# A mixture-of-experts layer: the last expert in the order is one of over 128 rows, and the norm of all tokens runs in pieces

## The chip, the core and the metric

One core of a Trainium2 chip runs the whole layer in one program. The metric is the time of one execution on the device in microseconds, the median of three runs. The profile is one further execution, taken by the hardware profiler. In the profile PE is TensorE's matrix products, PEld its weight loads, DVE VectorE, ACT ScalarE, POOL GpSimd and SP SyncE; L12 is line 12 of the kernel before.

## What is computed

A decoder layer for 512 tokens of width 1024: a token mixer (differential attention beside a gated branch), a norm, and then a mixture of 32 experts of which each token takes four. The end of the reference is what matters here:

```python
def moe_ffn(x, w_router, b_router, w_up, b_up, w_down, b_down):
    ...
    def expert_block(args):
        xb, e = args
        h = xb @ w_up[e] + b_up[e]
        gate, lin = h[:, :D_FF], h[:, D_FF:]
        gate = jnp.minimum(gate, SWIGLU_LIMIT)
        lin = jnp.clip(lin, -SWIGLU_LIMIT, SWIGLU_LIMIT)
        act = (lin + 1.0) * gate * jax.nn.sigmoid(SWIGLU_ALPHA * gate)
        return act @ w_down[e] + b_down[e]
    ...
# in reference():
x = layer_norm(DEEPNORM_ALPHA * x + mixed, ln1_g[l], ln1_b[l])
ffn = moe_ffn(x, w_router[l], b_router[l], w_up[l], b_up[l], w_down[l], b_down[l])
x = layer_norm(DEEPNORM_ALPHA * x + ffn, ln2_g[l], ln2_b[l])
```

The up weights of an expert are 8 MB, its down weights 4 MB.

## The kernel before

The first 290 us are the token mixer, the first norm and the routing. Then come the experts, in slots. An expert's rank by its number of tokens gives its capacity (`CAP_STEPS`, L35): the texts call an expert of at most 64 rows **narrow** (`L` in `ORDER`, L57), one of 72 to 128 rows **middle** (`M`) and one of 192 rows **wide** (`H`, the four fullest but for one fixed expert). `slot_order` (L61) takes the ranks in the order that `ORDER` writes out by hand. A middle expert multiplies with fp32r matmuls: each weight chunk is cast to a high part on ScalarE (L152) and its remainder is formed on VectorE (L153), into a ring of five buffers, and `full_mm` (L1342) makes six matmuls of 512 columns from it. A narrow expert multiplies the raw weights in f32, each row's two halves of 512 columns on the two halves of the array (`half_mm`, L1331): nothing is cast. A wide expert does both: 128 rows as a middle one and 64 more as a narrow one, the latter with PD as the place of its up product and X1 as that of its down product.

The work list (L1400 to L1405) is up(n), down(n-1), up(n+1), down(n) and so on; at its end stand down(N-2), up(N-1), down(N-1). It is cut into chunks (`stream`): 16 for an up product, 8 for a down product. Four chunks use one weight part of 2 MB; an expert has six parts, four up and two down. There are six raw buffers, and SyncE issues the next load when a buffer is released (`used`, L1563; `issue_load`, L1417): after the last split of a middle expert's part, after the last matmul of a narrow or wide one's. The program order on every engine is the order of emission (`manual_schedule`). Behind chunk c first the splits are emitted up to `limit(c + 1)` (L1591), which is three chunks ahead where something is hung in, then what `at(c, ...)` has hung in behind that chunk. So an instruction hung in behind chunk c stands on ScalarE and VectorE behind the splits of the next three chunks and ahead of all others.

Results are added to a tensor in DRAM, `accd`, which starts with the tokens themselves (L1121): `out_a` (L1310) scales an expert's rows by their gates into a buffer of `ys` and `out_b` (L1322) scatters them with an adding DMA of GpSimd (L1169, L1216). The last expert of before is narrow and different. Its gates are spread to all partitions (`last_diag`, `last_mm`, `last_gates`, L1655 to L1673) and multiplied into the transposed activations; the accumulator's rows for its tokens are gathered (`summed`, L1610) and put into its PSUM bank by a matmul with the identity (`last_start`, L1675), on which the down product then adds; so its PSUM holds finished sums. `last_rows` (L1680) takes their norm and scatters the result into the output. The norm of all tokens takes the accumulator without the last expert: `ln2_sums` behind the up product, `ln2_squares`, `ln2_scaled` and `ln2_out` behind the down product's second chunk (L1704 to L1711). It writes all 512 rows of the output, and the scatter of `last_rows` then overwrites those that the last expert has changed. `full_list` (L1183) makes the list of the last expert so that empty places repeat its first row. Behind the stream stands a loop over what did not fit the capacities (L1746), with no turn here.

Of the kernel before, what the change touches and what calls it, by code (L numbers as in the profile page):

```python
# [11 lines left out]
I32 = mybir.dt.int32  # L12
# [44 lines left out]
ORDER = "LMLHLMLMLMLHLMLMLMLHLMLMMLMLHLL"  # L57
assert "HH" not in ORDER and "MH" not in ORDER and ORDER[-1] == "L"
# [9 lines left out]
def moe_layer(ctx, tc, x, w_in, lambda_q1, lambda_k1, lambda_q2, lambda_k2, subln_g, gmlp_ln_g,  # L68
# [775 lines left out]

    def list_cols(lp, rows, dst=None):
# [326 lines left out]
    def transpose_h(src, eng, dst=None, js=slice(0, 4)):  # L1172

        if dst is None:
            dst = view(words(f"low{nxt('tb', 4)}", 1024), 0, 8, 64)
        tp = xbank().rearrange("p (j r) -> p j r", j=4)
        sv = src.rearrange("p (q j) -> p q j", j=4)
        for j in range(js.start, js.stop):
            nc.tensor.transpose(tp[:, j], sv[:, :, j], ident)
        eng(dst.rearrange("p (c j) r -> p j c r", c=2)[:, js], tp.rearrange("p j (c r) -> p j c r", c=2)[:, js])  # L1180
        return dst

    def full_list(s):  # L1183

        lp = xbank()[:, 0:8].rearrange("p (n c) -> p n c", n=2)
        for n in range(2):
            for i in range(NT):
                cols = tb.oh[:, i, 0:1].to_broadcast([128, 128]) if n else tb.oh[:, i]
                nc.tensor.matmul(lp[:, n], cols, tb.R[:, i, s], start=(n == 0 and i == 0), stop=(n == 1 and i == 3))
        cols_ = words("r0", 16)  # L1190
        t = view(cols_, 0, 2, 4)
        empty, gt, idx = (view(cols_, 8 + n, 1) for n in range(3))
        idx = idx.bitcast(I32)
        nc.vector.tensor_copy(t, lp)
        nc.vector.tensor_scalar(empty, t[:, 0, 1:2], -1.0, 1.0, op0=OP.mult, op1=OP.add)
        nc.vector.scalar_tensor_tensor(t[:, 0], t[:, 1], empty, t[:, 0], op0=OP.mult, op1=OP.add)
        nc.vector.scalar_tensor_tensor(idx, t[:, 0, 0:1], 2.0, bge[:, 2:3], op0=OP.mult, op1=OP.add)
        nc.vector.tensor_tensor(gt, t[:, 0, 2:3], t[:, 0, 3:4], op=OP.add)
        return idx, gt
# [21 lines left out]
    class Slot:  # L1221
# [3 lines left out]
        def __init__(self, n, s):  # L1225
# [8 lines left out]
            assert not (self.last and self.full)  # L1234
# [21 lines left out]
        def fetch(self, b):  # L1256
            if self.last:
                self.lists[b] = full_list(self.s)
            elif self.is_half(b):
# [20 lines left out]
        def t_a(self, b, hf):  # L1280
            if self.last:
                def gated(to, tp):
                    nc.vector.tensor_tensor(to, tp, tb.last_gates.unsqueeze(1).unsqueeze(1).to_broadcast([128, 2, 2, 64]),
                                            op=OP.mult)
                self.aT[b] = transpose_h(self.act_rows(b), gated, self.aT[b], slice(2 * hf, 2 * hf + 2))
            elif self.is_half(b):
# [7 lines left out]
        def act(self, b, q):  # L1294

            v = (self.act_rows(b),) + ((self.hg, self.hl) if self.is_half(b) else (PG[0:self.full], PL[0:self.full]))
            if self.last:
                return [a.rearrange("p (q j) -> p q j", j=4)[:, :, 2 * q:2 * q + 2] for a in v]
# [11 lines left out]
        def out_a(self):  # L1310
# [6 lines left out]
            for b in range(self.nparts):  # L1317
                half = self.is_half(b)
                self.y[b] = y_buf()[:, 0:512] if half else y_buf()[0:self.full]
# [11 lines left out]
        def half_mm(self, P, T, k, w, started=False):  # L1331
            for c in range(2):
                nc.tensor.matmul(P[64 * c:64 * c + 64], T[:, k], w[:, c * 512:(c + 1) * 512],  # L1333
                                 start=(k == 0 and not started), stop=(k == 7))
# [45 lines left out]
        def down_chunks(self):  # L1380
            out_ = []
            for k in range(KT):
                def mm(w, hi, lo, k=k):
# [4 lines left out]
                    if self.half:  # L1388
                        self.half_mm(self.hd, self.aT[-1], k, w, self.last)
# [137 lines left out]
    for n, sl in enumerate(slots):  # L1527
# [310 lines left out]
```

## Time and profile before

| | |
|---|---|
| median of three runs | 1448.32 us (1446.77 to 1450.57) |
| the profiled execution | 1449.89 us |
| its span, first to last instruction | 1448.2 us |
| TensorE busy, of the span | 1374.1 us (95%) |
| VectorE busy | 794.4 us (55%) |
| ScalarE busy | 602.5 us (42%) |
| moved by DMA | 461.47 MB |
| mean granted TensorE clock | 0.973 |

A row of the timeline reads: start, time taken, engine, line, operation, output and inputs by the program's names, shapes, count; in brackets the idle time of the engine ahead of it and what ended that. Rows of the same line that follow each other are merged (x32). A modelled end of a matmul overlaps the next one's start a little. A row of the windows gives, for a stretch, its length and each engine's busy time, then the granted clock, the share of time that the DMA engines were busy and what they moved.

### The profile page before, as it was taken

Reading aid. Unit: us, or ns where it says so; the run is one execution under the profiler, and the core shown is the slowest. Engines: PE = TensorE matmul, PEld = TensorE weight load, DVE = VectorE, ACT = ScalarE, POOL = GpSimd, SP = SyncE. Lnnn points to the kernel's source line nnn. Section 1 sums busy time; section 2 is a strip of 40 time slices with the busy share of each in tenths; the row PEclk is TensorE's granted clock in tenths of the full one; section 3 lists DMA queues with packets and bytes.
Section 4 is the critical chain, followed back from the end, with each engine's and each line's share of the span. In section 5 each row is a group of like instructions: output and inputs, shape, how many; then the busy total and the mean of one; then the engine's idle time right before and its main releaser. Section 6 shows DMA issues by size and latency. Waiting matters only on the chain. (4 is left out here: it accounts for less than half of the span.)

```text
span 1448.2 us, 16516 instructions
## 1 busy us (share of the span) xinstructions
PE 1374.1 (95%) x6282; PEld 808.7 (56%) x6282; DVE 794.4 (55%) x1207; ACT 602.5 (42%) x774; POOL 119.5 (8%) x130
## 2 busy tenths in 40 slices
PE   8999996989999999999999999999999999999973
PEld 6877775865654465564544564644454665554421
DVE  4455576675664464572725583835363785563304
ACT  3254453153552354461614362634252664352202
POOL 0000000022110010010100100110000011000010
PEclk9998998999999999999999999999999999999996
DMA  9020061488996989999978999999889999996964
GB/s 337 20 91 26 1 233 65 164 351 313 413 413 255 403 340 406 390 408 420 415 315 356 386 412 391 416 419 371 351 346 394 407 408 419 415 413 268 405 237 152
DMA packets 51411, 461.47 MB, mean 319 GB/s; under 512 B 7585, under 2 KB 8865, under 8 KB 26753
## 3 DMA queue, kind: packets, MB, share of 16 engines
q1 hardware_dynamic: 42800, 436.01, 73.8%
q0 software_dynamic: 8528, 24.39, 6.7%
q8 instruction: 50, 0.82, 0.2%
q14 instruction: 33, 0.26, 0.0%
HBM read 440.43 MB, written 19.94 MB: 318 GB/s over the span
## 5 line engine op out<-in xcount | busy, mean ns | idle before, releaser
L153 DVE TENSOR_TENSOR ring<-raw,ring 128x1024 fp32r<-128x1024 f32 (+1 forms) x400 | 466.4, 1211 | 147.9 <-ACT ring L152 147.3
L152 ACT CAST ring<-raw 128x1024 fp32r<-128x1024 f32 (+1 forms) x400 | 399.7, 1039 | 182.3 <-PE PG L1347 51.5
L1333 PE MATMUL PD<-raw,low 128*64 128x512 f32 x640 | 157.7, 608 | 0.3 <-ACT w L1320 0.2
L1347 PE MATMUL PD<-ring,bc 128*128 128x512 f32 (+7 forms) x512 | 147.1, 407 | 4.6 <-ACT ring L152 3.3
L1347 PE MATMUL PG<-ring,bc 128*128 128x512 f32 (+7 forms) x512 | 147.3, 409 | 0.6 <-ACT bc L971 0.5
L1347 PE MATMUL PL<-ring,bc 128*128 128x512 f32 (+7 forms) x512 | 146.7, 408 | 0.0
L153 DVE TENSOR_TENSOR low<-X,bc 128x512 fp32r<-128x512 f32 (+7 forms) x62 | 37.0, 596 | 189.3 <-ACT bc L152 189.2
L1333 PE MATMUL PG<-raw,low 128*64 128x512 f32 x512 | 133.6, 600 | 3.0 <-issue 2.0
L1333 PE MATMUL PL<-raw,low 128*64 128x512 f32 x512 | 132.5, 596 | 0.0
L1347 PEld LDWEIGHTS PD<-ring,bc 128*128 128x128 f32 (+7 forms) x512 | 81.8, 172 | 59.5 <-ACT ring L152 13.2
L1347 PEld LDWEIGHTS PG<-ring,bc 128*128 128x128 f32 (+7 forms) x512 | 84.5, 171 | 47.5 <-issue 18.7
L1347 PEld LDWEIGHTS PL<-ring,bc 128*128 128x128 f32 (+7 forms) x512 | 84.2, 171 | 47.0 <-issue 18.7
L1303 ACT ACTIVATE PG<-PG 128x512 f32<-128x512 f32 (+9 forms) x33 | 25.5, 772 | 167.7 <-PE PG L1347 96.7
L152 ACT CAST bc<-X 128x512 fp32r<-128x512 f32 (+7 forms) x62 | 31.7, 511 | 139.5 <-PE X L1206 139.5
L1304 DVE TENSOR_SCALAR w<-PL 128x512 f32<-128x512 f32 (+9 forms) x32 | 29.5, 923 | 100.1 <-PE PL L1347 68.6
L1347 PE MATMUL PG<-ring,low 128*128 128x512 f32 (+7 forms) x256 | 80.3, 395 | 0.3 <-DVE low L972 0.3
L1347 PE MATMUL PD<-ring,low 128*128 128x512 f32 (+7 forms) x256 | 80.0, 393 | 0.0
L1347 PE MATMUL PL<-ring,low 128*128 128x512 f32 (+7 forms) x256 | 80.0, 393 | 0.0
L1333 PEld LDWEIGHTS PD<-raw,low 128*64 128x64 f32 x640 | 37.9, 136 | 69.4 <-issue 65.1
L1333 PEld LDWEIGHTS PL<-raw,low 128*64 128x64 f32 x512 | 35.2, 136 | 61.0 <-issue 59.5
L1164 POOL DMA_INDIRECT w<-x1d,small x19 | 23.1, 1216 | 520.6 <-PE PG L1347 292.2
L1333 PEld LDWEIGHTS PG<-raw,low 128*64 128x64 f32 x512 | 33.4, 136 | 58.2 <-issue 50.7
(451 smaller groups left out, 1637.4 us busy)
## 6 DMA issues: line engine op xcount, KB each, us to landing
raw<-in_w_up_dram SPq DMA_DIRECT2D x128, 2048.0 KB, 16.1
raw<-in_w_down_dram SPq DMA_DIRECT2D x64, 2048.0 KB, 15.6
raw<-in_w_in_dram SPq DMA_DIRECT2D x8, 1024.0 KB, 9.4
raw<-in_w_o_dram SPq DMA_DIRECT2D x2, 2048.0 KB, 9.0
raw<-in_x_dram SPq DMA_DIRECT2D x4, 512.0 KB, 5.7
raw<-in_w_in_dram SPq DMA_DIRECT2D x4, 512.0 KB, 8.2
w<-in_x_dram SPq DMA_DIRECT2D x4, 512.0 KB, 3.9
x1d<-w SPq DMA_DIRECT2D x4, 512.0 KB, 2.8
```

Source lines behind the costliest of these rows:

```text
L152: nc.scalar.copy(hi, src)
L153: eng.tensor_tensor(lo, src, hi.bitcast(F32), op=OP.subtract)
L1164: nc.gpsimd.indirect_dma_start(out=xg, out_offset=None, in_=x1d_h, in_offset=bass.IndirectOffsetOnAxis(ap=idx, axis=0))
L1303: nc.scalar.activation(pg, pg, AF.Silu, scale=SWIGLU)
L1304: nc.vector.tensor_scalar(l, pl, LIMIT + 1.0, 1.0 - LIMIT, op0=OP.min, op1=OP.max)
L1333: nc.tensor.matmul(P[64 * c:64 * c + 64], T[:, k], w[:, c * 512:(c + 1) * 512], start=(k == 0 and not started), stop=(k == 7))
L1347: nc.tensor.matmul(P[0:self.full, cs], x_[:, k], w_[:, cs], start=(k == 0 and n == 0), stop=(k == 7 and n == 2))
```

## The change

The order is written anew so that the last expert is the wide one of the fourth rank; behind the second wide expert four narrow and middle pairs follow in place of three, and ahead of the last expert two narrow ones stand side by side. The last expert's list, gates and activations are those of any wide expert, except that the activations of its first 128 rows are made in two halves of 512 columns. Nothing is put under its down product. The rows of the accumulator for its tokens are gathered behind the down product of the expert before it (`summed`, two gathers), and `last_rows` adds its result to them on VectorE, writes the sums back and scatters the normed rows into the output, with a bound for empty places. The norm of all tokens is cut into pieces that are hung in behind single chunks of the last expert's up and down products. Its tiles stand in raw buffers, so that their load (`acc_load`) comes behind the up product's fifth chunk and behind the load of the gains (`ln2_load`). The narrow experts' scaled rows use halves of a buffer in turn (`y_half`).

```diff
-ORDER = "LMLHLMLMLMLHLMLMLMLHLMLMMLMLHLL"
-assert "HH" not in ORDER and "MH" not in ORDER and ORDER[-1] == "L"
+ORDER = "LMLHLMLMLMLHLMLMLMLMLHLMLMLMLLH"
+assert "HH" not in ORDER and "MH" not in ORDER and ORDER[-1] == "H"
...
+    def y_half():
+
+        h = nxt("yh", 2) * 512
+        return y_buf()[:, h:h + 512]
...
         if n == N - 1:
-            for hf in range(2):
-                at(c, lambda sl=sl, hf=hf: (sl.act_a(0, hf), sl.act_b(0, hf)), LEAD)
-            for hf in range(2):
-                at(c, lambda sl=sl, hf=hf: sl.t_a(0, hf), LEAD)
+            at(c, lambda sl=sl: (sl.act_a(0, 0), sl.act_b(0, 0), sl.act_a(1), sl.act_b(1)), LEAD)
+            at(c, lambda sl=sl: (sl.t_a(0, 0), sl.t_a(1, 0)), LEAD)
+            at(c, lambda sl=sl: (sl.act_a(0, 1), sl.act_b(0, 1)), LEAD)
+            at(where[(n, "d", 1)], lambda sl=sl: sl.t_a(0, 1), LEAD)
...
+    accr = [view(W, 1024, 1024), view(W, 0, 512)]
+    zl = [act2[0], act2[1][:, 0:512]]
+    unused = view(W, 3584, 512).bitcast(BF16)
 
     def summed():
...
+        for b, d in enumerate((accd, accd_h)):
+            nc.gpsimd.indirect_dma_start(out=accr[b], out_offset=None, in_=d,
+                                         in_offset=bass.IndirectOffsetOnAxis(ap=slots[-1].lists[b][0], axis=0))
+
+    def acc_load():
+        tb.xo = view(raw_tile(), 0, 4, 1024)
         for i in range(NT):
             nc.sync.dma_start(tb.xo[:, i], accd[i * 128:(i + 1) * 128])
...
+    def ln2_sum(i):
+        nc.scalar.activation(unused, tb.xo[:, i], AF.Copy, accum_out=tb.sums[:, 0, i:i + 1])
+        nc.vector.tensor_scalar_mul(mv1[:, i, 0:1], tb.sums[:, 0, i:i + 1], 1.0 / D)
+        nc.vector.tensor_scalar_mul(tb.sums[:, 1, i:i + 1], tb.sums[:, 0, i:i + 1], -1.0 / D)
+
+    def ln2_square(i):
+        nc.scalar.activation(unused, tb.xo[:, i], AF.Square, bias=tb.sums[:, 1, i:i + 1], accum_out=tb.sums[:, 2, i:i + 1])
+
+    def ln2_places():
+        tb.no = view(raw_tile(), 0, 4, 1024)
+
+    def ln2_scaled(i):
+        nc.vector.scalar_tensor_tensor(tb.no[:, i], tb.xo[:, i], mv1[:, i, 0:1], ln2[:, 0], op0=OP.subtract, op1=OP.mult)
+
+    def ln2_scale():
+        nc.vector.tensor_scalar(nv1, tb.sums[:, 2], 1.0 / D, EPS, op0=OP.mult, op1=OP.add)
+        nc.vector.tensor_scalar_mul(nv1, nv1, -0.5)
+        rsqrt(rs1, nv1, t1)
+
+    def ln2_out(i):
+        layer_norm_out(tb.no[:, i], i, None, ln2[:, 1], 1)
+        nc.sync.dma_start(out[0][i * 128:(i + 1) * 128], tb.no[:, i])
+
+    out_h = out[0].rearrange("r (c f) -> (r c) f", c=2)
+
+    def last_rows(sl):
+        r0_ = words("r0", 16)
+        m = view(r0_, 0, 2, 2)
+        v, y, t, pm = (view(r0_, 4 + 2 * n, 2) for n in range(4))
+        idx = [l[0] for l in sl.lists]
+        nc.vector.scalar_tensor_tensor(accr[1], sl.hd, sl.lists[1][1], accr[1], op0=OP.mult, op1=OP.add)
+        nc.vector.bn_stats(st1[:, 0], accr[1])
+        nc.vector.bn_aggr(m[:, 1], st1[:, 0])
+        both = X0[:, 0:2]
+        nc.tensor.matmul(both, tb.pair, m[:, 1], start=True, stop=True)
+        nc.vector.scalar_tensor_tensor(accr[0], PD, sl.lists[0][1], accr[0], op0=OP.mult, op1=OP.add)
+
+        for b, d in ((1, accd_h), (0, accd)):
+            nc.gpsimd.indirect_dma_start(out=d, out_offset=bass.IndirectOffsetOnAxis(ap=idx[b], axis=0), in_=accr[b],
+                                         in_offset=None)
         for c in range(2):
...
+            nc.vector.bn_stats(st1[:, c], accr[0][:, c * 512:c * 512 + 512])
+        nc.vector.bn_aggr(m[:, 0], st1)
+
+        nc.vector.tensor_copy(pm, both)
+        nc.vector.tensor_tensor(t[:, 0:1], m[:, 1, 0:1], pm[:, 0:1], op=OP.subtract)
+        nc.vector.scalar_tensor_tensor(v[:, 1:2], t[:, 0:1], t[:, 0:1], pm[:, 1:2], op0=OP.mult, op1=OP.add)
+        nc.vector.tensor_copy(v[:, 0:1], m[:, 0, 1:2])
         nc.vector.tensor_scalar(v, v, EPS, -0.5, op0=OP.add, op1=OP.mult)
         rsqrt(y, v, t)
...
+        for b, (mean, g, bb, d, top) in enumerate(((m[:, 0, 0:1], ln2[:, 0], ln2[:, 1], out[0], S),
+                                                   (pm[:, 0:1], tb.ln2h[:, 0], tb.ln2h[:, 1], out_h, 2 * S))):
+            nc.vector.scalar_tensor_tensor(zl[b], accr[b], mean, g, op0=OP.subtract, op1=OP.mult)
+            nc.vector.scalar_tensor_tensor(zl[b], zl[b], y[:, b:b + 1], bb, op0=OP.mult, op1=OP.add)
+            nc.gpsimd.indirect_dma_start(out=d, out_offset=bass.IndirectOffsetOnAxis(ap=idx[b], axis=0), in_=zl[b],
+                                         in_offset=None, bounds_check=top - 1, oob_is_err=False)
+
     at(where[(N - 2, "d", "sum")] + 1, summed, L)
     at(where[(N - 1, "u", 2)], ln2_load, LEAD)
-    at(where[(N - 1, "u", "sum")], ln2_sums, LEAD)
-    for f in (ln2_squares, ln2_scaled, ln2_out):
-        at(where[(N - 1, "d", 1)], f, LEAD)
+    at(where[(N - 1, "u", 4)], acc_load, LEAD)
+    at(where[(N - 1, "u", 6)], ln2_start, LEAD)
+    at(where[(N - 1, "u", 9)], ln2_places, LEAD)
+    for i in range(NT):
+        at(where[(N - 1, "u", 8 + i)], lambda i=i: ln2_sum(i), LEAD)
+        at(where[(N - 1, "u", 9 + 2 * i)], lambda i=i: ln2_scaled(i), LEAD)
+        at(where[(N - 1, "u", 12 + i)], lambda i=i: ln2_square(i), LEAD)
+        at(where[(N - 1, "d", 3 + i)], lambda i=i: ln2_out(i), LEAD)
+    at(where[(N - 1, "d", 2)], ln2_scale, LEAD)
```

Left out above are the removed `full_list`, `last_diag`, `last_mm`, `last_gates`, `last_start` and the old `ln2_*` functions, whose lines the section before names, and the branches of `Slot` that called them.

## Rows read from the trace of the kernel before

**Rows 1.** Windows: stretch, length, busy us by engine, granted clock, DMA share, GB/s

```profile
1018.30:1328.70 310.40, 310.40 (x1406) 163.32 (x1406) 183.19 (x219) 146.50 (x165) 27.81 (x20) 1.00 0.96 386
...
1401.80:1415.30 13.50, 0.00 (x0) 0.00 (x0) 1.61 (x4) 3.69 (x7) 2.57 (x2) 0.64 0.63 198
```

**Rows 2.** Timeline of TensorE, ahead of the last down product

```profile
1415.36 1.97 PE L1678 MATMUL PD<-w,ident 128*64 128x512 f32 x4 [13.58 <-DMA w<-accd,r]
...
1418.49 7.42 PE L1333 MATMUL PD<-raw,low 128*64 128x512 f32 x32
```

**Rows 3.** Timeline of VectorE and GpSimd, the last expert's rows

```profile
1431.59 0.69 DVE L1684 BATCH_NORM_STATS2 small<-PD 128x6 f32<-128x512 f32 x1
...
1437.46 0.96 POOL L1701 DMA_INDIRECT out_dram<-ring,r  x1 [3.28 <-DVEq L1746]
```

**Rows 4.** Line 1701, the last scatter into the output

```profile
DMA to landing us min/median/max: 3.0/3.0/3.0
```

**Rows 5.** Timeline, the end of the fourth wide expert's up product

```profile
1331.54 1.08 PE L1333 MATMUL PD<-raw,low 128*64 128x512 f32 x4
...
1334.27 0.75 PE L1179 MATMUL X<-ident,w 128*128 128x128 f32 x4
...
1334.84 0.69 DVE L1308 SCALAR_TENSOR_TENSOR w<-PD,w 128x512 f32<-128x512 f32 x1
```

**Rows 6.** Timeline of TensorE, a middle, a wide and a narrow expert

```profile
1276.08 1.15 PE L1347 MATMUL PD<-ring,bc 128*72 128x512 f32 x4
...
1288.69 1.07 PE L1347 MATMUL PG<-ring,bc 128*128 128x512 f32 x4
...
1315.43 1.19 PE L1347 MATMUL PG<-ring,bc 128*128 128x512 f32 x4
...
1323.21 1.05 PE L1189 MATMUL X<-r,oh 128*128 128x4 f32 x8
...
1380.01 7.09 PE L1333 MATMUL PD<-raw,low 128*64 128x512 f32 x32 [0.20 <-ACT w L1320]
```

**Rows 7.** Timeline of ScalarE, behind the second wide expert

```profile
815.03 1.00 ACT L1303 ACTIVATE PG<-PG 96x1024 f32<-96x1024 f32 x1 [5.26 <-PE PG L1347]
...
899.79 2.94 ACT L152 CAST ring<-raw 128x1024 fp32r<-128x1024 f32 x3 [7.36 <-DMA raw<-in_w_down_dram]
...
936.16 1.00 ACT L1303 ACTIVATE PG<-PG 88x1024 f32<-88x1024 f32 x1 [5.34 <-PE PG L1347]
...
964.10 2.94 ACT L152 CAST ring<-raw 128x1024 fp32r<-128x1024 f32 x3 [10.11 <-DMA raw<-in_w_down_dram]
```

**Rows 8.** Timeline of TensorE, the third middle expert's down product there

```profile
965.19 0.70 PE L1347 MATMUL PD<-ring,bc 128*88 128x512 f32 x2 [1.65 <-ACT ring L152]
966.45 0.69 PE L1347 MATMUL PD<-ring,bc 128*88 128x512 f32 x2 [0.56 <-DVE ring L153]
```

**Rows 9.** Timeline of ScalarE and SyncE, the norm's tiles and gains

```profile
1411.49 1.06 ACT L1630 ACTIVATE ring<-bc 128x1024 f32<-128x1024 f32 x1 [8.30 <-DMA bc<-accd]
...
1412.38 1.12 SPq L1623 DMA_DIRECT2D w<-in_ln_b_dram  x2
1412.45 0.19 ACT L1630 ACTIVATION_READ_ACCUMULATOR ring<-bc 128x1 f32 x1
...
1416.08 1.06 ACT L1630 ACTIVATE ring<-bc 128x1024 f32<-128x1024 f32 x1 [0.66 <-DMA bc<-accd]
```

**Rows 10.** DMA issues: out<-in, queue, count, KB each, median us to landing

```profile
raw<-in_w_up_dram SPq DMA_DIRECT2D x128, 2048.0 KB, 16.1
...
w<-in_ln_b_dram SPq DMA_DIRECT2D x2, 128.0 KB, 8.9
```

**Rows 11.** Waits: who for whom, us in total, times, longest

```profile
POOL accd L1169 <- DMA accd<-w,small: 36.7, 3, 12.3
```

**Rows 12.** Timeline of VectorE, the root and last pass of all tokens

```profile
1424.60 0.17 DVE L183 TENSOR_SCALAR small<-small 128x4 int32<-128x4 int32 x1
...
1426.80 4.87 DVE L753 SCALAR_TENSOR_TENSOR ring<-ring,small,w 128x1024 f32<-128x1024 f32 x4
```

More of the change, by code (lines that the diff above doesn't have):

```diff
@@ L1170, in scatter_h, with transpose_h @@
                                      in_=y, in_offset=None, compute_op=OP.add)
-    def transpose_h(src, eng, dst=None, js=slice(0, 4)):
-        if dst is None:
-            dst = view(words(f"low{nxt('tb', 4)}", 1024), 0, 8, 64)
+    def transpose_h(src, eng):
+        dst = view(words(f"low{nxt('tb', 4)}", 1024), 0, 8, 64)
         tp = xbank().rearrange("p (j r) -> p j r", j=4)
         sv = src.rearrange("p (q j) -> p q j", j=4)
-        for j in range(js.start, js.stop):
+        for j in range(4):
             nc.tensor.transpose(tp[:, j], sv[:, :, j], ident)
-        eng(dst.rearrange("p (c j) r -> p j c r", c=2)[:, js], tp.rearrange("p j (c r) -> p j c r", c=2)[:, js])
+        eng(dst.rearrange("p (c j) r -> p j c r", c=2), tp.rearrange("p j (c r) -> p j c r", c=2))
         return dst
[L1183 to L1199, printed above, removed]
     def transpose_half(dst, src, hf, rows):
@@ L1233, in __init__ @@
             self.last = n == len(order) - 1
-            assert not (self.last and self.full)
+            assert self.wide or not self.last
             self.parts = [0, 128] if self.wide else [0]
@@ L1280, in t_a @@
         def t_a(self, b, hf):
[L1281 to L1286, printed above, removed]
+            if self.is_half(b):
                 if hf == 0:
@@ L1296, in act @@
             v = (self.act_rows(b),) + ((self.hg, self.hl) if self.is_half(b) else (PG[0:self.full], PL[0:self.full]))
-            if self.last:
-                return [a.rearrange("p (q j) -> p q j", j=4)[:, :, 2 * q:2 * q + 2] for a in v]
+            if self.last and b == 0:
+                return [a[:, q * 512:q * 512 + 512] for a in v]
             return v
@@ L1318, in out_a @@
                 half = self.is_half(b)
-                self.y[b] = y_buf()[:, 0:512] if half else y_buf()[0:self.full]
+                self.y[b] = y_half() if half else y_buf()[0:self.full]
                 nc.scalar.activation(self.y[b], self.hd if half else PD[0:self.full], AF.Copy, scale=self.lists[b][1])
@@ L1664, in last_diag @@
         nc.vector.tensor_scalar_mul(tb.pair, tb.pair, 0.5)
-    def last_mm():
-        tb.last_ps = xbank()[:, 0:64]
-        nc.tensor.matmul(tb.last_ps, one[0:64].to_broadcast([64, 128]), view(tb.last_t, 0, 64, p=64), start=True, stop=True)
-    def last_gates():
-        tb.last_gates = view(tb.last_t, 64, 64)
-        nc.vector.tensor_copy(tb.last_gates, tb.last_ps)
-    def last_start():
-        for c in range(2):
-            nc.tensor.matmul(slots[-1].hd[64 * c:64 * c + 64], ident[:, 64 * c:64 * c + 64], tb.accr, start=True, stop=False)
```

73 lines of the change are left out of this document (9 added, 64 removed).

## The prediction

> **What bounds the kernel now.** I read the windows first, then the last stage on TensorE, then what the casts waited for. In the expert stages TensorE is never free: from the third wide expert to the fourth it is busy 310.40 of 310.40 us, and the DMA engines are busy 0.96 of that time [rows 1]. Two resources are nearly full at once, so the order of the experts decides which of them is late. At the end that changes: from 1401.8 TensorE does nothing, because the matmul that puts the accumulator's rows under the last down product (last_start) waits 13.58 us for the gather of those rows [rows 1, 2]. The first down matmul starts at 1418.49, and the 32 take 7.42 us [rows 2]. VectorE is then still at the norm of all tokens and turns to the last expert's rows at 1431.59; their scatter starts at 1437.46 and lands 3.0 us later [rows 3, 4]. What follows up to 1448.2 stays as it is.
>
> **The end of the up product.** Removed: 1401.8 to 1418.49, 16.7 us. In its place stands the wait for a wide expert's activations, which no other product covers now. In the wide expert of before the linear half can be clipped when PL is complete, 1.0 us ahead of the end of the last half-row matmuls (1331.54 + 1.08); a product of 512 columns takes 0.69 on VectorE, the four clips and products 2.75, a group of transposes 0.75 [rows 5]. So the down product starts 2.75 - 1.0 + 0.1 + 0.75 = 2.6 us after the up product. Bounds: 1.5 (two groups of transposes alone) and 4.5 (nothing starts early). Gain 14.1. The wide expert's third group goes between its down products (+0.7); three groups of the fourth wide expert leave the stream (-2.0), one of the last narrow expert enters it (+0.7): -0.6. The broadcast of the gates and half of the eight small matmuls of the list go (the eight took 1.05; estimate 1.0 for both), and a narrow down product that took 7.42 behind the idle time takes 7.09 elsewhere [rows 2, 6]: -1.3.
>
> **The order of the experts.** Here the change pays. A weight part is 2 MB, an expert has six, six buffers hold them, and a narrow expert uses its parts up faster than parts land. Behind the second wide expert the casts of the middle experts' down weights wait longer each time: 7.36 us for their DMA at 899.79, 10.11 at 964.10 [rows 7]; the second of these is the third middle expert's, and there TensorE waits too, 1.65 and then 0.56, 2.2 in all [rows 8]. Between the two landings lie twelve parts: 64.31 us, 5.36 a part. TensorE wants such a pair every (936.16 - 815.03) / 2 = 60.57 us [rows 7]. So each pair loses 3.7 us, and only a wide expert gives it back. The new order puts four pairs, not three, behind the second wide expert: +3.7. Behind the third, two middle experts stood side by side and TensorE had no wait at all [rows 1]; now there are three pairs, which end with the wait of 2.2 once more, and two narrow experts follow directly. From the down weights of the last middle expert to the first up weights of the wide one ten parts have to land: 53.6 us. TensorE's work between them: a middle down product 12.6 less two groups of transposes, 11.8; a narrow up product 14.9 (1387.10 to 1401.8, the broadcast replaced by a group); a narrow down 7.1 with four groups, 9.8; another 7.1 [rows 2, 6]. Sum 43.6. It waits 10.0. Together 3.7 + 2.2 + 10.0 = 15.9; bounds 6 (lighter traffic of gathers and scatters makes up the pairs' lack) and 20.
>
> **The norm in pieces.** The first sum on ScalarE is emitted behind the cast that is three chunks ahead, and everything later is queued behind it there: the next casts, and so the products, and the activations. It waits for the accumulator's first tile, which SyncE issues behind the last weights and behind the gains of the norm, these two now the other way round. Counted from the landing of the wide expert's first up part: its products start after 2.2 (the wait in rows 8), a chunk is 2.59 (three from 1315.43 to 1323.21 [rows 6]), so the up product ends at 43.6 and the down product could start at 46.2. The last weights land at 5 x 5.36 = 26.8. The gains took 5.8 behind the last accumulator tile (from 1416.08 to 1421.9, which is the second of two issues at 1412.38 and its 8.9 to landing), a tile 1.5 (1411.49 to 1416.08, three steps) [rows 9, 10]. So the first tile lands at 34.1. From there ScalarE has seven casts of 1.0 [rows 7], four sums and three squares of 1.26 (1.06 and the read of the sum [rows 9]) ahead of the first Silu: 15.8, at 49.9. Another 4.7 (a subtraction 1.22, four operations of 0.69, a group of transposes) lead to the down product: 54.6 instead of 46.2. +8.4. Bounds: 0, where the tile lands by 26, and 10.
>
> An up part of 2 MB had 16.1 us from issue to landing [rows 10]: a transfer on this queue pays for what is ahead of it. The Trainium skill, page "DMA: Bandwidth & Descriptors", section "Anatomy of one DMA", gives a DMA a fixed 2.0 us and its bytes at 436 GB/s. By that the tile would land some 3.2 us after its issue (an estimate from that page), the hold would be nothing, and the time that of rival 2.
>
> The two gathers of the accumulator's rows, on GpSimd behind the last narrow scatter, have the whole wide up product as cover: nothing. A scatter waits for the one before it to land, up to 12.3 us [rows 11]; with halves of y ScalarE needn't wait for it as well: nothing, since that wait is covered now too. The scaling of all tokens (four passes of 1.22 [rows 12]) and the four writes to the output lie beside down products of 20.7 us, in which VectorE has 16.7 to do (five subtractions 6.1, the rest of the norm 8.4, activations 2.2): nothing, and 4.9 if that cover is gone.
>
> **The tail.** Before: last matmul 1425.91, landing 1440.46, 14.55 us [rows 2 to 4]. After, on a free VectorE: product and statistics of the half 1.6; of the full rows 1.22, twice 0.69 and 0.2; five small operations 1.0; the root 2.2 (1424.60 to 1426.80); two passes of 1.22, and gaps 0.3: 10.4 [rows 3, 12]. The first output scatter lands 3.0 to 3.6 later. The second writes the same tensor, and as on the accumulator I let it wait for that landing [rows 11]: 14.0 + 3.0 = 17.0. +2.5. Bounds: +0.6 (no wait) and +4 (the bounds check, which no row prices).
>
> **Sum.** -14.1 - 0.6 - 1.3 + 15.9 + 8.4 + 2.5 = +10.8. The profiled execution took 1449.89 with a span of 1448.2; the median of three is 1448.32. On the median: 1459.1 us.
>
> **Rivals.** 1. The weights keep up, and the change does what it looks like: the idle time goes, everything else hides. -14.1 - 0.6 - 1.3 + 2.5 gives 1434.8. It holds where a part takes no more than 60.57 / 12 = 5.05 us. For it: the waits of TensorE are small so far. Against it: 5.36 in the saturated pair. The Trainium skill, page "DMA: Bandwidth & Descriptors", section "Specifications", gives a ceiling of 435 GB/s, by which a part takes 4.8 us (an estimate) and this rival would hold; the trace's 5.36 are 391 GB/s of weights, with gathers and scatters between them. 2. The weights run dry as forecast, but the tiles arrive in time: without the hold 1450.7, no difference. For it: casts run three chunks ahead, which is 7.8 us of lead. Against: the tiles can't be issued before a buffer of the wide expert is free, behind its fourth chunk, when three parts are still on their way. 3. All costs at their upper bounds, 20, 10 and 4, the wide expert's own parts late too: 1466.3.
>
> **How the numbers follow.** This kernel's measurement can tell about 0.3%, 4.3 us, from no change. Forecast 0.50, rival 1 0.14, rival 2 0.21, rival 3 0.15. The likeliest is 1459.1. The range 1444 to 1467 leaves out rival 1 and the far end of rival 3. Faster by over 0.3% is rival 1: 0.14. Within is rival 2: 0.21. Slower is the forecast and rival 3: 0.65.
>
> **What would show it.** In the profile of after, TensorE's idle time ahead of the last down product falls to some 7 us, with a wait of about 4 inside the wide up product; narrow matmuls and casts wait for weight DMAs behind the fourth pair (about 4) and from the last middle expert to the wide one (about 12); ScalarE sits before the first sum until a landing. If the waits for weights aren't there, the step on the order is wrong and rival 1 holds; if they are, but the sums start on time, the hold is wrong. The second output scatter should start after the first has landed; if it starts right behind it, the tail is 2 us too long.

## The result, and the profile after

The changed kernel takes 1457.7 us (median of five, 1456.9 to 1459.6) beside 1449.0 of the kernel before: 1.0057 times its time, interval 1.0042 to 1.0072. Four more runs, on the chip of runs 5 to 8 below, gave 1.0068 (1.0051 to 1.0086). The prediction was 1459.1. The profiled execution has a span of 1455.3, 7.1 more than before's.

Spans alone hide some of it. What comes ahead of the experts is the same in both kernels, but took 3.3 us less in the profiled execution of after. Two timelines of TensorE, the routing's transposes, before and then after (line numbers in a run's rows are those of its own kernel):

```profile
297.43 0.48 PE L1075 MATMUL X<-ident,r 128*128 128x128 f32 x1 [3.19 <-DVE r L835]
```

```profile
294.15 0.48 PE L1080 MATMUL X<-ident,r 128*128 128x128 f32 x1 [3.20 <-DVE r L835]
```

From there to the end it is 1150.8 before and 1161.2 after: **+10.4**. All profiled executions are compared below from this point. The changed kernel, profiled a second time (run 8), takes 1163.0 from there, so a difference of under 2 us between two such totals means nothing until rows show where it lies.

Where the difference arises is told by the windows of both kernels from the third middle expert behind the second wide one (the same product in both, [rows 8]) to the last matmul. Columns as in [rows 1]. Before, cut where the last up product ends:

```profile
965.19:1401.80 436.61, 435.05 (x1946) 220.66 (x1946) 233.66 (x279) 188.15 (x213) 37.25 (x26) 1.00 0.94 377
1401.80:1425.91 24.11, 10.45 (x40) 3.31 (x40) 8.96 (x23) 9.93 (x17) 2.57 (x2) 0.72 0.56 174
```

After, cut at the last wide expert's first product and at the end of its up product:

```profile
962.44:1353.49 391.05, 379.79 (x1721) 190.82 (x1721) 201.45 (x255) 161.52 (x185) 37.83 (x26) 1.00 0.98 396
1353.49:1404.60 51.11, 46.60 (x168) 21.26 (x168) 27.33 (x33) 26.39 (x34) 4.43 (x3) 0.93 0.74 275
1404.60:1429.15 24.55, 22.62 (x93) 11.49 (x92) 19.64 (x32) 8.11 (x11) 0.00 (x0) 1.00 0.21 86
```

TensorE's idle time ahead of the last expert's up product rises from 1.56 to 11.26 (length less busy time); inside that product it is 4.51; behind it 1.93 in place of 13.66. So idle time is moved, not saved: 17.7 us beside 15.2. TensorE's busy time in these windows is 449.01 beside 445.50, and its clock is 0.93 in the last up product. Behind the last matmul stand 26.15 us in place of 22.29.

The rows that answer to those of before, in the timeline of TensorE after. The fourth pair behind the second wide expert (with the pattern of [rows 8]), the third middle expert behind the third, the way from there to the wide one, the wait inside its up product, and the start of the last down product ([rows 2]):

```profile
1021.37 1.08 PE L1312 MATMUL PG<-raw,low 128*64 128x512 f32 x4 [0.91 <-DMA raw<-in_w_up_dram]
1027.35 0.69 PE L1326 MATMUL PD<-ring,bc 128*80 128x512 f32 x2 [1.65 <-ACT ring L152]
1028.61 0.69 PE L1326 MATMUL PD<-ring,bc 128*80 128x512 f32 x2 [0.57 <-DVE ring L153]
...
1304.46 0.86 PE L1155 MATMUL X<-r,oh 128*128 128x4 f32 x4 [1.91 <-DVE oh L1147]
...
1353.49 0.73 PE L1326 MATMUL PG<-ring,bc 128*128 128x512 f32 x2 [3.22 <-ACT ring L152]
1354.75 0.99 PE L1326 MATMUL PG<-ring,bc 128*128 128x512 f32 x2 [0.53 <-DVE ring L153]
...
1391.09 0.73 PE L1326 MATMUL PG<-ring,bc 128*128 128x512 f32 x2 [3.46 <-ACT ring L152]
...
1407.79 1.18 PE L1326 MATMUL PD<-ring,bc 128*128 128x512 f32 x4
```

The wait that [rows 2] showed is gone; the last up product ends at 1404.60 and the down product starts 3.2 us later. In place of the 13.58 stand many waits of 0.5 to 3.5 us. ScalarE tells whom they are for; its timeline, the cast of the third middle expert's down weights, of the wide one's first up part, and the first sum of the norm:

```profile
1299.04 2.94 ACT L152 CAST ring<-raw 128x1024 fp32r<-128x1024 f32 x3 [7.29 <-DMA raw<-in_w_down_dram]
...
1352.39 2.94 ACT L152 CAST ring<-raw 128x1024 fp32r<-128x1024 f32 x3 [9.58 <-DMA raw<-in_w_up_dram]
1355.23 0.68 ACT L1299 ACTIVATE k<-X,small 128x512 f32<-128x512 f32 x1
...
1388.96 1.06 ACT L1619 ACTIVATE w<-raw 128x1024 bf16<-128x1024 f32 x1 [14.28 <-DMA raw<-accd]
```

The third middle expert's cast waits 7.29 us, and TensorE feels it at another place than forecast: not at the product, but at the next list, whose mask stands on VectorE behind the late splits (1.91 for `oh`). The first sum waits 14.28 us for the accumulator's tile, and everything behind it on ScalarE waits too.

The clock, in windows of after: the stretch of a short wait and the product behind it, then the two long waits, each with the chunk behind it:

```profile
960.70:962.44 1.74, 0.05 (x2) 0.00 (x1) 0.02 (x1) 1.10 (x2) 0.00 (x0) 1.00 0.99 424
962.44:966.50 4.06, 3.50 (x17) 2.29 (x17) 3.99 (x8) 3.56 (x5) 0.00 (x0) 1.00 1.05 448
...
1350.27:1353.49 3.22, 0.00 (x1) 0.01 (x1) 0.03 (x1) 1.10 (x2) 0.00 (x0) 1.00 1.06 383
1353.49:1358.69 5.20, 4.67 (x13) 1.74 (x13) 4.66 (x5) 4.49 (x6) 2.21 (x1) 0.67 1.00 429
1387.63:1391.09 3.46, 0.01 (x2) 0.00 (x0) 0.23 (x3) 2.13 (x4) 0.00 (x0) 1.00 0.83 334
1391.09:1396.07 4.98, 4.45 (x10) 1.57 (x10) 4.81 (x8) 4.98 (x9) 0.00 (x0) 0.66 0.03 13
```

A chunk of the wide up product takes 2.6 us [rows 6]; behind each long wait the first one takes 5.0 to 5.2 at a mean clock of 0.67, that is at 1.2 GHz for most of it. Behind the wait of 1.74 the clock stays at 1.00 here; run 8 shows that this isn't so in every execution.

### The profile page after: what moved, and what is told of

It reads as the page before. It is cut to its first block, busy times and chain, and to the rows that moved or that the text cites. A ratio compares the mean times of both kernels' runs of the same rounds, so it can differ in the third digit from the quotient of the medians.

```text
span 1455.3 us, 16510 instructions
## 1 busy us (share of the span) xinstructions
PE 1373.7 (94%) x6272; PEld 804.3 (55%) x6272; DVE 799.8 (55%) x1218; ACT 599.7 (41%) x772; POOL 123.4 (8%) x132
## 4 chain that ended last, share of the span: by engine, by line
PE 81%; DMA 10%; DVE 5%; ACT 2%; issue 1%; POOL 0%; POOLq 0%; SPq 0%; DVEq 0%; ACTq 0%
PE PD L1326 13%; PE PG L1326 12%; PE PL L1326 11%; PE PD L1312 8%; PE PG L1312 6%; PE PL L1312 6%; DMA raw<-in_w_down_dram 6%; PE X L1312 4%; PE X L1192 2%; DMA raw<-in_w_up_dram 2%; PE X L1183 2%; DVE ring L153 2%; DMA raw<-accd 1%; PE PD L820 1%; PE PL L560 1%
## 5 line engine op out<-in xcount | busy, mean ns | idle before, releaser
L1282 ACT ACTIVATE PG<-PG 128x512 f32<-128x512 f32 (+8 forms) x33 | 25.5, 772 | 154.3 <-PE PG L1326 90.5
L1283 DVE TENSOR_SCALAR w<-PL 128x512 f32<-128x512 f32 (+8 forms) x32 | 29.5, 922 | 92.2 <-PE PL L1326 66.4
L1169 POOL DMA_INDIRECT w<-x1d,small x20 | 26.2, 1309 | 535.6 <-PE PG L1326 287.3
## 6 DMA issues: line engine op xcount, KB each, us to landing
raw<-in_w_up_dram SPq DMA_DIRECT2D x128, 2048.0 KB, 16.7
```

What stands on the lines that cost most here:

```text
L1169: nc.gpsimd.indirect_dma_start(out=xg, out_offset=None, in_=x1d_h, in_offset=bass.IndirectOffsetOnAxis(ap=idx, axis=0))
L1282: nc.scalar.activation(pg, pg, AF.Silu, scale=SWIGLU)
L1283: nc.vector.tensor_scalar(l, pl, LIMIT + 1.0, 1.0 - LIMIT, op0=OP.min, op1=OP.max)
```

## Why the tile is late: the queue of SyncE

SyncE's timeline of after, from the last weights on:

```profile
1345.55 5.08 SPq L675 DMA_DIRECT2D raw<-in_w_down_dram  x2
1350.81 0.34 SPq L1605 DMA_DIRECT2D w<-in_ln_g_dram  x1
1368.37 1.19 SPq L1607 DMA_DIRECT2D k<-in_ln_g_dram  x2
1369.68 0.51 SPq L1605 DMA_DIRECT2D w<-in_ln_b_dram  x1
1370.24 1.10 SPq L1607 DMA_DIRECT2D k<-in_ln_b_dram  x2
1373.57 11.07 SPq L1600 DMA_DIRECT2D raw<-accd  x4
```

`ln2h` (L1607) is written over a `y` that the last narrow scatter still reads. SyncE stands from 1351.2 to 1368.4 before it may issue that load, and the tiles come behind it. The scatter itself is late: its rows are scaled at 1355.23, on ScalarE behind the cast that waited 9.58 for weights, it is issued at 1356.19 and lands some 12.2 later. That looks like the cause, but the landings say otherwise. SyncE's wait for the scatter, in after and then in run 1 (columns as in [rows 11]), and the landing of `ln_g` (L1605) in after:

```profile
SPq L1607 <- DMA accd<-k,small: 17.1, 1, 17.1
...
SPq L1600 <- DMA accd<-k,small: 17.1, 1, 17.1
...
DMA to landing us min/median/max: 33.0/33.0/33.0
```

`ln_g` was issued ahead of that wait, at 1350.81, and landed at 1383.8 all the same, 3.5 behind the last weights, for which SyncE's second tile waits until 1380.28. And the tiles read the accumulator that the scatter writes, so they wait for it wherever they stand: in run 1, where `ln2h` is behind them, SyncE stands the same 17.1 us. Run 9, with the loads in the order of after, has a landing for each: the last weights 1379.6, `ln_g` 1382.6, `ln_b` 1385.7, the last of `ln2h` 1386.7, the first tile 1387.9. So the chain is late weights, the gains behind them on the same queue, the tile (15.4 from its issue), the sum. That the scatter makes the tile later is not shown for after.

## Experiments

The runs are told with their ratio to before and, from their profile, the time from the routing's transposes to the end (before 1150.8, after 1161.2).

**1. The tiles ahead of the gains.**

```diff
-    at(where[(N - 1, "u", 2)], ln2_load, LEAD)
+    at(where[(N - 1, "u", 2)], ln2_gain, LEAD)
     at(where[(N - 1, "u", 4)], acc_load, LEAD)
+    at(where[(N - 1, "u", 5)], ln2_load, LEAD)
```

`ln2_gain` loads `ln_g` alone; `ln_b` and both halves of `ln2h` are left to `ln2_load`.

> Edit: SyncE issues the accumulator's tiles ahead of ln2h and ln_b instead of behind them; the gain ln_g stays in front, since the scaling on VectorE needs it. In the changed kernel SyncE stands from 1350.8 to 1368.4, because ln2h is written over a y that the last narrow scatter still reads; the first tile is issued at 1373.57 and lands at 1388.96, 36.6 us behind the first up part. Theory (the hold is the queue in front of the tiles): the tiles are issued at about 1368.5, land by 1384 at the latest, the first sum starts before ScalarE's next cast is due, TensorE's waits of 3.46 and 0.53 inside the wide up product go, and with them the chunk that took 5.0 instead of 2.6 behind them: -6.4, some 1451.3. Rival (the tile lands when the last weights have landed, wherever it stands on the queue): first sum at 1387 or later, at most -1.5. Second rival (the lost time is the wait alone, the slow chunk is something else): -4.0.

Measured: 1155.2, so -6.0. The timed runs spread from 1452.3 to 1458.4 (ratio 1.0049, 1.0032 to 1.0066), which by themselves would not tell -6 from -2, and the profiled execution is the fastest of the six; but its trace shows where the time goes. SyncE and ScalarE, and then TensorE's first down product:

```profile
1369.13 1.76 SPq L1600 DMA_DIRECT2D raw<-accd  x4
...
1384.24 1.06 ACT L1622 ACTIVATE w<-raw 128x1024 bf16<-128x1024 f32 x1 [8.93 <-DMA raw<-accd]
...
1403.08 1.18 PE L1326 MATMUL PD<-ring,bc 128*128 128x512 f32 x4
```

The tile lands 6 us earlier, counted from the routing, and TensorE's wait of 3.46 inside the up product is gone. The first theory holds: the gains in front of the tiles are the hold. Run 7, which has this edit too, has its first sum 5.2 earlier than after. One more thing shows: the down product starts 18.84 us behind the first sum, as in after (1388.96 to 1407.79: 18.83). The chain from the tile still sets it.

**2. The half rows' output first.**

```diff
-        for b, (mean, g, bb, d, top) in enumerate(((m[:, 0, 0:1], ln2[:, 0], ln2[:, 1], out[0], S),
-                                                   (pm[:, 0:1], tb.ln2h[:, 0], tb.ln2h[:, 1], out_h, 2 * S))):
+        for b, mean, g, bb, d, top in ((1, pm[:, 0:1], tb.ln2h[:, 0], tb.ln2h[:, 1], out_h, 2 * S),
+                                       (0, m[:, 0, 0:1], ln2[:, 0], ln2[:, 1], out[0], S)):
```

> Edit: the last expert's half rows are scaled and written out ahead of its full rows. Theory (the second output scatter waits for the landing of the first, and the first, of 512 KB, has the longer landing): the scatter of the half rows is issued 1.1 us earlier than the first one is now (two passes of 0.75 instead of two of 1.28), at about 1438.6, lands in some 2.1 to 3; the full rows are ready at about 1441.0, the second scatter waits under 1 us and lands 4.1 later: -0.8 to -1.3 at the end of the profiled execution, with no other change before the last matmul. Rival (the two don't wait for each other's landing, GpSimd is just slow to issue): the second scatter again starts 4.9 behind the first and the end moves by less than 0.3.

Measured: 1160.0, so -1.2; ratio 1.0053 (1.0033 to 1.0072). GpSimd after, and then in this run:

```profile
1439.67 1.26 POOL L1672 DMA_INDIRECT out_dram<-w,small  x1 [4.93 <-DVE w L1671]
1444.52 1.00 POOL L1672 DMA_INDIRECT out_dram<-w,small  x1 [3.59 <-DMA out_dram<-w,small]
```

```profile
1439.34 1.79 POOL L1672 DMA_INDIRECT out_dram<-w,small  x1 [3.86 <-DVE w L1671]
1443.04 0.99 POOL L1672 DMA_INDIRECT out_dram<-w,small  x1 [1.90 <-DMA out_dram<-w,small]
```

The second scatter waits for the first's landing in both. In after the first one brings 512 KB and lands 4.07 behind its start. From the last matmul to the end this run takes 24.5 us in place of 26.15, 1.6 less, and its first sum came 0.4 later than in after, so the total shows 1.2. The theory holds, with a little more than it forecast.

**3. Another order of the experts.**

```diff
-ORDER = "LMLHLMLMLMLHLMLMLMLMLHLMLMLMLLH"
+ORDER = "LMLMLLHLMMLMLLHLMMLMLLHLLMLMMLH"
```

> Edit: the order of the experts alone, LMLMLLHLMMLMLLHLMMLMLLHLLMLMMLH: the wide ones come later, two narrow ones stand ahead of each of the first three, and no more than one narrow-middle pair follows another without a wide expert near. Theory (the weights run dry because of where the wide experts stand): the waits of 8.2 us more than before, and 2.4 of half clock behind the longest of them, go: -8 to -11, some 1447 to 1450; the hold and the tail stay as they are. Rival (with a wide expert at the end the last bytes land as late as ever, so the waits only move): the sum of TensorE's waits for casts and weights stays over 12 us and the time within 3 us of 1457.7.

Measured: 1448.6 us, ratio 0.9995 (0.9976 to 1.0013); 1151.3, so -9.9. TensorE's waits of over 0.25 us, from 60 us behind the routing's transposes to the first product of the last expert, sum to 8.4 in place of 17.2 (in before 6.3), none longer than 2.04, but the hold is there, 2.75 us. The theory holds, and with the order alone the change costs nothing against before. In the windows of this run the clock falls behind 2.75 us of idle time too:

```profile
1377.50:1380.28 2.78, 0.03 (x2) 0.00 (x1) 0.24 (x3) 2.14 (x4) 0.00 (x0) 1.00 0.97 389
...
1383.00:1385.50 2.50, 2.50 (x6) 0.84 (x3) 2.33 (x5) 2.50 (x6) 0.00 (x0) 0.50 0.00 0
```

**4. Less to load for the last two narrow experts.**

```diff
+        if n in (N - 3, N - 2) and kind == "u" and part % 2:
+            raw_of[(n, kind, part)] = raw_of[(n, kind, part - 1)]
+            return
```

> Edit: the last two narrow experts load only the first and third of their four up parts; the products of the second and fourth read the part before them, so these two experts' rows are computed with wrong weights, with the same instructions on TensorE. That takes 4 parts (8 MB, 21 us at 5.3 us a part) from the DMA queue just where TensorE waits. Theory (the weights run dry between the last middle expert and the wide one): the waits of 1.31, 1.10, 3.22 and 0.53 go, and so does the stretch in which the first wide chunk took 5.2 instead of 2.6: -8.7; the weights of the wide expert land earlier too, so the tile of the accumulator finds an empty queue, lands some 4 us after its issue at about 1369, and the hold goes as well: -6.4. Together some 1442.6. Rival (ScalarE's order, not the weights, holds the first wide cast): the wait of 3.22 stays, and the gain is under 4. Second rival (the hold is SyncE's wait for the scatter and its issue, not the queue): -8.7 alone, 1449.

Measured: 1441.9 us, ratio 0.9952 (0.9937 to 0.9966); 1142.9, so -18.3, more than the 15.1 expected. From 964 to the end of the up product TensorE has only the fourth pair's waits left. The scaling of the last narrow rows isn't held by a cast any more, and SyncE and ScalarE follow:

```profile
1365.97 2.61 SPq L1603 DMA_DIRECT2D raw<-accd  x4
...
1373.86 1.06 ACT L1622 ACTIVATE w<-raw 128x1024 bf16<-128x1024 f32 x1 [7.68 <-DMA raw<-accd]
```

The tile lands 7.9 behind its issue in place of 15.4 (some 4 were expected, but the gains are still ahead of it). The rivals, ScalarE's own order and a hold that is SyncE's alone, fall: weights cause both the waits and most of the hold. With the weights early SyncE's wait for the scatter does count: it ends at 1362.8, behind the last weights (1360.7), and the tile lands 13.1 behind these, where run 9 has 8.3. Beyond the 15.1 go the 1.9 of the list mask, whose splits are in time now, and 0.5 of the gap behind the up product (2.6 in place of 3.2); 0.8 stays unassigned.

**5. All three edits together.** The edits of 1, 2 and 3 in one kernel.

> Edit: the three edits that gained together: the order of the experts of the third run, the accumulator's tiles ahead of ln2h and ln_b, the half rows' output ahead of the full ones'. Theory (weights, hold and tail are three separate costs, each on the path): from the 1445.6 of the profiled run with the new order go its wait of 2.75 and 0.53 and the half-clock stretch behind them, some 2.3, and 0.9 of the tail: span 1439, median some 1441, faster than before by 0.5%. Rival (with the order mended the tile's landing is covered or another wait comes up behind it): 1445 or more, no difference from before.

Measured: 1444.0 us, ratio 0.9961 (0.9948 to 0.9974); 1144.8, so -16.4 where the three alone sum to -17.1. It is faster than before, by 0.4% where 0.5% (some 1441) was expected. TensorE at the end of the up product:

```profile
1392.47 1.08 PE L1312 MATMUL PD<-raw,low 128*64 128x512 f32 x4
1394.13 0.75 PE L1192 MATMUL X<-ident,w 128*128 128x128 f32 x4 [0.58 <-DVE w L1287]
1395.69 0.75 PE L1183 MATMUL X<-ident,w 128*128 128x128 f32 x4 [0.81 <-DVE w L1287]
1396.19 1.18 PE L1326 MATMUL PD<-ring,bc 128*128 128x512 f32 x4
```

Here the gap is 2.6 (1393.55 to 1396.19), as forecast for a free chain, and the down product starts 21.2 behind the first sum: the tile no longer sets it.

**6. The kernel before with another order.**

```diff
-ORDER = "LMLHLMLMLMLHLMLMLMLHLMLMMLMLHLL"
+ORDER = "LMLLHLLMMLHLMMLMMLLHLMMLLHLMLML"
```

> Edit: the kernel before, with another order of the experts alone (LMLLHLLMMLHLMMLMMLLHLMMLLHLMLML, it ends in a narrow one as before does). Theory (before too loses where narrow-middle pairs follow each other, TensorE's waits for casts and weights there are 1.65, 0.56, 1.1, 0.8 and smaller ones at two places, some 6.5 in all, and its 13.58 at the end waits for the accumulator and not for weights): -3 to -6, some 1443 to 1445. Rival (before's waits are small change and its end stays): within 2 of 1448.3.

Measured: 1436.1 us, ratio 0.9906 (0.9889 to 0.9924); 1138.7, so -12.1. Two to four times what was expected: besides the waits for weights the large idle time shrank, and the theory was wrong to leave it out. TensorE, as [rows 2], and GpSimd:

```profile
1402.24 1.98 PE L1678 MATMUL PD<-w,ident 128*64 128x512 f32 x4 [5.03 <-DMA w<-accd,r]
```

```profile
1371.30 1.57 POOL L1169 DMA_INDIRECT accd<-k,small  x1 [31.71 <-ACT k L1320]
1383.83 1.51 POOL L1216 DMA_INDIRECT accd<-w,small  x1 [10.95 <-ACT w L1320]
1395.20 1.02 POOL L1613 DMA_INDIRECT w<-accd,r  x1 [9.87 <-DMA accd<-w,small]
```

In before two scatters of the fourth wide expert and one of a narrow one stand directly ahead of the gather, each behind the landing of the one before ([rows 11]: 12.3). Here only one does. 5.03 is left of 13.58, so 8.6 of the 12.1 is this wait; the other 3.5 is within what was expected of the waits for weights.

**7. Filling the wait.** The kernel of 1, with products that nobody reads in the idle time ahead of the wide expert's first chunk.

```diff
+    def busy_fill():
+        fp = X0
+        for _ in range(11):
+            nc.tensor.matmul(fp, onehot[0:96, 1:2].to_broadcast([96, 128]), tb.bup[0:96, 0:512], start=True, stop=True)
+
+    at(where[(N - 2, "d", "sum")], busy_fill, LEAD)
```

> Edit: the first run of this study (tiles first) with eleven bias products of 128x512 into a bank that nobody reads, some 2.4 us, directly ahead of the wide expert's first chunk, where TensorE has nothing to do for 3.14 us. Theory (TensorE falls to half its clock behind an idle time of that length, and that makes the first wide chunk 5.1 instead of 2.6): the wait shrinks to about 0.7, the first products start at the same time, the chunk takes 2.6 at a granted clock of 1.00, and the last matmul ends 2.4 earlier: span 1448.2. Rival (the first chunk is slow because its operands come late, one split after the other): it takes 5 us again and nothing moves.

Measured: 1454.7 us, ratio 1.0028 (1.0014 to 1.0042); 1157.5, which is no gain on the 1155.2 of run 1. The window of the first two chunks (its length runs into the second):

```profile
1356.35:1361.60 5.25, 4.72 (x20) 2.38 (x20) 4.62 (x4) 4.37 (x6) 2.20 (x1) 1.00 1.01 427
```

The clock stays at 1.00 and the first chunk ends at 1359.96, 3.6 us long in place of 5.2 in after and 5.1 in run 1. So the half clock is real, and it costs 1.6 of the 2.6 that were put down to it; the rest is the wait of 0.53 for a split, which is the rival's cause, and the bias products that the first chunk has and others don't. And the time is not earlier for it: the down product starts 18.85 behind the first sum as ever. The up product ends earlier and the gap behind it grows (2.95 in place of 1.91 for the activations); behind that one the clock falls once more, and the time from the first sum to the end is 67.9 in place of run 1's 66.4. The first sum itself came 0.8 later than in run 1. The start of the down product:

```profile
1403.30 0.75 PE L1192 MATMUL X<-ident,w 128*128 128x128 f32 x4 [2.95 <-DVE w L1287]
...
1405.13 1.92 PE L1326 MATMUL PD<-ring,bc 128*128 128x512 f32 x4
```

**8. The changed kernel again.**

> The changed kernel itself, to have its times on the same chip as the others: 1457.7, give or take 1.5, and in its trace the same waits, 3.2 and 3.46 with the slow chunks behind them.

Measured: 1459.5 us (1459.1 to 1464.7). Its profiled execution was the longest of the four, 1163.0 from the routing on. The waits were 2.42 and 5.40 in place of 3.22 and 3.46; the first sum came at 1396.58 and the down product at 1415.41, again 18.83 later. Counted from the routing the first sum is 1.9 later than in after, which is the whole difference. The waits shift, the chain doesn't.

The clock fell at other places than in after. Windows from the end of a wait of 1.53, and from the end of the one of 2.42:

```profile
1034.09:1040.00 5.91, 5.34 (x18) 3.18 (x19) 5.84 (x10) 4.39 (x6) 1.12 (x1) 0.71 1.01 432
...
1360.74:1366.50 5.76, 5.23 (x22) 2.60 (x24) 4.73 (x5) 4.55 (x6) 1.87 (x1) 1.00 1.03 415
```

It fell behind the short wait (and, in this run, behind waits of 1.74 and 1.92), and not behind the longer one, whose first wide chunk took 3.6 us, as long as in run 7. So the price of 1.6 for a chunk is seen a second time, and the length of a wait alone doesn't tell whether it is paid.

**9. Less to load for the narrow expert of the fourth pair.** The edit of run 4 for slot 21 alone.

> Edit: the narrow expert of the fourth pair behind the second wide one loads only the first and third of its up parts; its second and fourth products read the part before them, so that one expert's rows are computed with wrong weights, with the same instructions. Theory (each pair more behind a wide expert costs what its weights lack): the waits of 0.91, 1.65 and 0.57 around 1021 to 1029 go, -3.1 there, those around 956 to 964 (1.44, 1.69, 0.56) stay, and nothing comes back before the last wide expert: 1158 instead of 1161.2 from the routing's transposes to the end. Rival (later waits grow by what is saved here, since the queue has to bring the same bytes): the last matmul moves by less than 1.

Measured: 1454.4 us, ratio 1.0043 (1.0028 to 1.0058); 1156.7, so -4.5. TensorE runs through 1015 to 1035 without a wait, and those of 959 to 967 are as they were (1.52, 1.69, 0.55):

```profile
1015.00:1035.00 20.00, 20.00 (x98) 9.78 (x95) 11.92 (x17) 8.90 (x12) 0.99 (x1) 1.00 1.02 413
```

The theory holds: the rival's giving back isn't seen, since the tile lands that much earlier as well (1090.4 behind the routing's transposes in place of 1094.8). The 1.4 beyond the forecast 3.1 isn't shown to be the edit's, as the two profiles of the changed kernel are 1.8 apart.

## Why the prediction was right, point by point

It was right in the total (+10.8 forecast; +10.4 in the trace, +8.7 in the medians) and in the mechanisms. In the sizes, order and hold were too high, the tail too low, the small matmuls gained nothing, and the clock was missing. That the total came within 0.4 of the trace is in part luck: these errors offset each other.

- **The idle time ahead of the down product**: forecast -14.1, measured 16.7 to 3.2, -13.5. The 2.6 is what activations that nothing holds take (run 5: 2.6); the rest is the hold.
- **Transposes and small matmuls**: forecast -1.9, measured nothing. By groups of one shape in the two long stretches the transposes lie 0.2 lower and the products of lists and gates 0.1 higher.
- **The order**: forecast 3.7 + 2.2 + 10.0 = 15.9. The fourth pair cost 3.1 (run 9 takes away 4.5 at the end). The third middle expert cost 1.9, by way of the list mask, and the last stretch 6.2 (1.31, 1.10, 3.22 and 0.53). With 0.5 that after has lost by 964, less 1.0 of other waits of before that are gone, the waits come to 10.7; the half-clock chunk adds 1.6: 12.3. The mis-sized term is the last, 10.0. Its transfers were right: ten parts between the two casts took 53.4 (1299.04 to 1352.39; forecast 53.6). Its work was not: from the third middle down product, at 1300.67, to the first wide chunk TensorE needed 52.8 with 7.5 of waits in them, so 45.3 of work, where 43.6 was forecast. And the 1.9 at the list is among these 7.5, while the forecast had its 2.2 ahead of that stretch.
- **The hold**: forecast 8.4. Inside the up product TensorE waited 3.46 and 0.53, and the chunk behind took 1.9 more than 2.6 and that 0.53: 5.8; run 1 gives 6.0. The path was the one worked out. Counted from the landing of the first up part, the last weights, the last gain and the first tile land at 27.6, 34.7 and 35.8 in run 9 (forecast 26.8, 32.6 and 34.1). In after the first sum starts at 36.6 and the down product 18.8 later (forecast 15.8 + 4.7 = 20.5), at 55.4, where 54.6 was forecast. The mis-sized term is the free case beside it: without the hold the up product ends at 46.3 (run 1) and not at 43.6, mainly because its first chunk is 2.5 slow. The 3.2 us from issue to landing that the prediction sets against this, as an estimate from the Trainium skill, page "DMA: Bandwidth & Descriptors", section "Anatomy of one DMA", is for one DMA alone, and that section gives its fit for DMAs issued by GpSimd. The case's own rows have 3.7 for a tile in before, issued by SyncE when the last weights had landed, and 15.4 here behind weights and gains.
- **The tail**: forecast +2.5, measured +3.8: from the last matmul to the issue of the last output scatter 15.37 in place of 11.55, and 10.8 from there to the end in both. The first scatter came as forecast, 10.5 behind the last matmul (10.4). Mis-sized was its landing: 3.0 was the landing of the 256 KB of [rows 4]; 512 KB took 4.07, and 0.8 passed before GpSimd started the next.
- **Not in the sum: the clock.** Two chunks at half clock, 1.6 and 1.9, which stand in the terms of the order and the hold. The 1.6 is measured (runs 7 and 8); the 1.9 is what is left of the second chunk's time, and no run tests it alone.

-13.5, -0.1, +12.3, +5.8 and +3.8 make +8.3 of the +10.4; most of the remaining 2 is in the products: the same 1712 matmuls take 477.7 us in place of 472.7, summed over groups of one shape, and only 3.5 of these 5.0 are the clock's. No single row of the rest is large enough to assign.

One thing the sum got wrong in kind. It adds order and hold as if both stood on TensorE. They hang on one queue: weights that are late hold the casts, the last of them hold the gains and the tile, and the tile sets the end. From the first sum to the end it is 66.3 to 66.5 us in after and in runs 1, 4, 8 and 9, whatever TensorE waited for; in runs 3 and 7, where the clock fell behind the up product too, it is 67.5 and 67.9. That is why the end of run 9 moved with its tile, and why run 7, which filled a wait and left the tile where it was, gained nothing.

Neither rival 1 (1434.8, weights keep up) nor rival 2 (1450.7, no hold) nor rival 3 (1466.3, all at the upper bounds) came true. Run 3 comes nearest to rival 1, with the hold left in, and is still 0.5 above before in the trace; run 1 is rival 2: 4.4 above before in the trace, where rival 2 had 2.4. That the order also sets before's idle time, by the scatters that stand ahead of its gather, was in no case. Run 6 shows that most of this idle time could be had for an edit of one line, with the last expert narrow.

## What to carry to other kernels

An idle time that a profile puts down to one DMA is often the end of a chain of ordered DMAs: look at what stands ahead of it (here adding scatters, some 12 us each) before rebuilding the consumer. Costs that hang on each other through queues don't add: find the one landing that sets the end, count from it, and expect that time saved elsewhere turns into a longer wait. When a load is moved, list what stands ahead of it on its queue: here the last weights and the gains set when the tile landed, and the long wait of the engine that issued it, which catches the eye, is not shown to have done so.

## What the runs showed of the hardware

- TensorE's granted clock fell from 1.00 to 0.50, that is from 2.4 to 1.2 GHz, with each of the longer waits of TensorE in these traces: during those of 13.58 (before), 5.03 and 5.40 (runs 6 and 8), and within the first products behind those of 2.75 to 3.46. The first chunk behind waits of 3.1 to 3.5 has a mean of 0.66 to 0.69 (after, runs 1 and 2). Behind shorter waits it differs from one execution to the next: in after it stayed at 1.00 behind 1.69, 1.65 and 1.91, in run 8 it fell behind 1.74, 1.53 and 1.92 and stayed at 1.00 behind 2.42. In before the clock was 0.64 in the long idle time [rows 1], and the product behind it lost 0.3, 7.42 beside 7.09 [rows 2, 6]; in run 6, with the same two groups of matmuls between the idle time and the product, it took 8.51. The Trainium skill, page "TensorE: Matmul & The Clock Gate", Part 1: The HAM clock gate, says that the throttled state is the default and that activity releases it; the rows agree, with 1.2 GHz behind a wait and 2.4 GHz again within the next chunks.
- An adding scatter into the accumulator that is issued among weight loads takes about 12 us to land (in before a median of 11.9 over those of L1169, and 4.7 for the last one, issued when all weights had landed), and the next access of that tensor stands behind it. The Trainium skill, page "DMA: Bandwidth & Descriptors", Rules for kernel authors, asks for such a wait, since an accumulate reads its destination and writes it later; what it costs here is in the rows alone.
- Loads that SyncE issued landed in the order of their issue (runs 1, 3, 4 and 9, from the last weights on). The first accumulator tile, 512 KB, took 3.7 us to land with nothing ahead of it (before), 7.9 behind the gains (run 4) and 14.7 to 15.4 behind weights (runs 1 and 9, after).
